# A trunk of two mixed-attention layers: first weights by row block, the memory rows' norm moved, forget parts earlier, last weave 8 to 6

## The chip, the core and the metric

The kernel runs on one core of a Trainium2 chip. TensorE (PE) multiplies matrices, VectorE (DVE) and ScalarE (ACT) work elementwise, GpSimd (POOL) does little here, and SyncE (SP) issues the DMAs. Each engine takes its instructions strictly in its own order; a semaphore holds one back until what it reads is there. The metric is the device time of one execution in microseconds (us); fewer is better.

## The reference

A hybrid decoder trunk with sequence 512 (T), model width 1024 (D) and two layers. In each layer:

```python
h = RMSNorm(x);  p = h @ w_in            # one projection, 10 kinds of heads and gates
y_a = DSA   (lightning-indexer top-k, gathered keys, low-rank KV, rotary)
y_b = FoX   (causal attention, logits + cum[t] - cum[s], cum = cumsum(log_sigmoid(p['fox_f'] + b)))
y_c = stick-breaking attention (sb_q, sb_k, sb_v)
y_d = NSA   (compressed / selected-block / window branches, gated)
y_e = cross-attention into mem: k, v = RMSNorm(mem) @ w_mem_kv     # 256 memory rows
merged = sum_n sigmoid(p['merge'][n]) * ((y_n * silu(z_n)) @ w_branch[n])
x = x + merged @ w_out
```

A last RMSNorm follows the two layers. Each branch has four heads of width 64; all is float32.

## The kernel before, in words

x lies transposed: 8 tiles of 128 features by 512 tokens. Each large projection is taken as three matmuls of a high and a low part (hi·hi, lo·hi, hi·lo; `mm3`, L261 to L264, all recorded at L259). So each weight block of 128x1024 (512 KB) is loaded into a buffer `wraw` (L278), split by ACT into `whi` (L269) and by DVE into `wlo` (L270). The raw buffers are a ring of two (tag "raw"), which the memory rows `mraw` (L1218) share with the weights.

A layer is written as generators: each `yield` ends a piece of work, and `weave` (L658) takes pieces in turn from several of them, the next one always from the generator whose pieces taken, divided by its number n, are fewest. `chain` runs generators one after another and `take` a few pieces of one. This order of writing and a priority decide how a scheduler lays out each engine's list; within a list nothing overtakes.

- The start of layer 0, `first` (L695) with `begin_tile` (L678): sb_q of the unnormed x, one tile after another: `u` and `ul` are the high and low parts of x times the norm's gain, `sq` its square, and the first weights are split by `start_split` (L707, ACT at L711, DVE at L712). Both weight blocks are 128x1024 and lie by column tile. Then `sumsq` and `rsqrt4` (a Newton iteration of twelve small DVE steps, L297 to L309), while sb_v's weights (ACT at L735, DVE at L736) are split.
- `memory_rows` (L375), layer 0 only: the memory rows' squares (ACT L336), seven adds (DVE L342), `ssq`, `rsqrt4`, `rowb` (PE L317) and the copy `rmem` (ACT L381). Layer 1 uses the same `rmem`. `mem_proj` (L1214) scales the rows by `rmem` (DVE L1222), splits them into `yhi` and `ylo` (L269, L270) and multiplies them with memk (two blocks) and memv (two).
- `small_proj` (L814): small heads; `smt_p` are transposes of rows of the tile `v` (L829), `sw_p` the rotary swap, then the logarithm of the forget gates (`fe`, `fu`, `forget_gates` L874).
- The stages (L1373 to L1400): stick-breaking pair 0 (`sb_attn(0)`, tiles `sbz`, `sp`, `Yc`) woven with the silu gate, the small projections and the memory projections; pair 1; then memory, NSA, DSA and FoX attention, each woven with the projections of the next and the merge of the branch before.
- `forget_rows` (L886), called once for each pair of FoX heads: splits the cumulative gates into `chi` and `clo`, loads a table `cbt` (L892), casts it to `sel` (ACT L894) and adds them to queries and keys by the matmuls `fox_e`.

Of the kernel before, what the change touches and what calls it, by code (L numbers as in the profile page):

```python
# [103 lines left out]
def _layout(x, mem, positions, norm_g, w_in, kv_norm, w_uk, w_uv, fox_bias, nsa_pe_k, nsa_pe_v,  # L104
# [82 lines left out]
def trunk(ctx: ExitStack, tc: tile.TileContext, xt, memt, pos, wall, small, vec, ca, cb, out):  # L187
# [32 lines left out]
    START_W = (1, 3)  # L220
    start_w = []
    for k in range(KT):
        nc.sync.dma_start(xs[:, k], xt[:, k])
        if k in START_W:
            r = wts.tile([128, 1024], F32, name="wraw", tag="raw", bufs=2)
            nc.sync.dma_start(r, wall[0, CH[('sb_q', 0)], :, 1024 * len(start_w):1024 * len(start_w) + 1024])
            start_w.append(r)
# [444 lines left out]
    def begin_layer(l):  # L672

        U = [wk.tile([128, 2, T], F32R, name="u", tag=t, bufs=2) for t in ("yhi", "yhi", "ylo", "ylo", "Z", "Z")]
        u = [x[:, e] for x in U for e in range(2)]
        return SimpleNamespace(uh=u[:KT], ul=u[KT:] + [slot("ul", F32R) for _ in range(2 * KT - len(u))], sq=[])

    def begin_tile(b, l, k, x, inorder=lambda e, ins: ins, middle=lambda k: None):  # L678

        sq = slot("sq")  # L680
        g = vcol(l * V_L + V_NG + k)
        inorder(0, nc.scalar.activation(b.uh[k], x, AF.Copy, scale=g))
        middle(k)
        inorder(0, nc.scalar.activation(sq, x, AF.Square))
        inorder(1, nc.vector.scalar_tensor_tensor(b.ul[k], x, g, f32(b.uh[k]), op0=OP.mult, op1=OP.subtract))
        if k == 0 or (l and k == KT - 1):
            b.sq.append(sq)
        else:
            inorder(1, nc.vector.tensor_add(b.sq[0], b.sq[0], sq))

    def layer(l, xs, begin):
# [3 lines left out]
        def first():  # L695
# [4 lines left out]
            if l == 0:  # L700
# [5 lines left out]

                def start_split(k):  # L707
                    if k in START_W:
                        w = [wts.tile([128, 1024], F32R, name="w", tag=t, bufs=3) for t in ("whi", "wlo")]
                        r = start_w[START_W.index(k)]  # L710
                        inorder(0, nc.scalar.activation(w[0], r, AF.Copy))  # L711
                        inorder(1, nc.vector.tensor_sub(w[1], r, f32(w[0])))  # L712
                        ws.append(w)
# [350 lines left out]
        def nsa_proj():  # L1064
# [22 lines left out]
            ht = sm.tile([64, 128], F32, name="ht", bufs=1)  # L1087
# [292 lines left out]
        if l == 0:  # L1380
            run(chain(memory_rows(), take(sp1, 1)))
# [3 lines left out]
            weave((sb_attn(0), 8), (chain(silu2('sb_z', lv.ZC), take(ixp, 1), take(sp1, 1), take(ixp, 1), mp), 10))  # L1385
# [12 lines left out]
        weave((fox_attn(), 16), (merge(0, lv.YA), 8))  # L1398
# [37 lines left out]
```

## Time and profile before

| | |
|---|---|
| median of 3 runs | 1337.55 us (1336.85 to 1339.21) |
| profiled execution, its span | 1338.58 us, 1336.8 us |
| mean granted clock of PE | 0.995 of full |
| busy: PE, DVE, ACT | 97%, 69%, 50% of the span |
| chain that ended last | PE 81%, ACT 9%, DVE 6%, issue 3%, DMA 1% |
| DMA | 124.10 MB, mean 93 GB/s |

Times in the timelines are us from the start of the span. In a row a tile's name stands for what is written, and after the arrow for what is read; matmuls overlap, so the distance of two starts says how fast they follow each other, not the length of one. An idle time in brackets is that of the engine before the row, with what ended it.

### The profile page before, as it was taken

What the parts mean: (1) busy time and instruction counts of PE and PEld (TensorE: products, weight loads), DVE (VectorE), ACT (ScalarE), POOL (GpSimd) and SP (SyncE); (2) the same over time, 40 slices, a digit from 0 to 9 for tenths busy, and PEclk for the clock granted to TensorE, in tenths of its full rate; (3) what the DMA queues carried; (4) which work ended last, traced back from release to release, by engine and by line L of the source; (5) the groups of instructions that cost most, each with busy time, mean ns of one, the idle gap of its engine ahead of it and who ended that gap; (6) DMA issues with size and microseconds to landing.
All of it is one profiled execution on the core that took longest, in us unless ns stands there. A gap on an engine that the chain in (4) does not pass through costs nothing.

```text
span 1336.8 us, 18894 instructions
## 1 busy us (share of the span) xinstructions
PE 1299.8 (97%) x7160; PEld 1066.1 (80%) x7160; DVE 916.1 (69%) x1983; ACT 675.0 (50%) x1260; POOL 42.5 (3%) x60
## 2 busy tenths in 40 slices
PE   7999999999999899999999999999999999999997
PEld 6777777878888788878887777778778878887896
DVE  6887999768655545644567799995686563465554
ACT  6887834357545424434447695534574452343340
POOL 0000011000000000000000001111000000000000
PEclk9999999999999999999999999999999999999998
DMA  6432321321223122223523213222122222323231
GB/s 222 135 127 79 103 90 62 95 78 60 65 78 103 55 95 79 69 83 130 184 88 126 96 63 127 79 70 89 49 78 63 88 87 69 100 81 99 95 111 63
DMA packets 40235, 124.10 MB, mean 93 GB/s; under 512 B 4432, under 2 KB 6480, under 8 KB 40144
## 3 DMA queue, kind: packets, MB, share of 16 engines
q1 hardware_dynamic: 40144, 122.89, 28.4%
q8 instruction: 56, 0.92, 0.3%
q14 instruction: 35, 0.29, 0.1%
HBM read 118.16 MB, written 4.72 MB: 92 GB/s over the span
## 4 chain that ended last, share of the span: by engine, by line
PE 81%; ACT 9%; DVE 6%; issue 3%; DMA 1%; SPq 0%; DVEq 0%; ACTq 0%
PE pj L259 67%; PE Y L259 4%; PE S L259 3%; PE pt L556 3%; ACT whi L269 2%; PE sbz L259 1%; DVE wlo L270 1%; ACT sw L430 1%; ACT Qi L854 1%; ACT sw L431 1%; ACT sp_t L388 1%; DVE Kl L456 0%; DVE rt L435 0%; DVE sw L434 0%; DMA wraw<-in_wall_dram 0%
## 5 line engine op out<-in xcount | busy, mean ns | idle before, releaser
L259 PE MATMUL pj<-h_hi,whi 128*128 128x512 f32 x1088 | 430.2, 397 | 1.1 <-DVE rt L433 1.1
L259 PE MATMUL pj<-h_lo,whi 128*128 128x512 f32 x1088 | 428.3, 394 | 0.0
L259 PE MATMUL pj<-h_hi,wlo 128*128 128x512 f32 x1088 | 426.7, 392 | 0.0
L270 DVE TENSOR_TENSOR wlo<-wraw,whi 128x1024 fp32r<-128x1024 f32 x183 | 223.6, 1222 | 216.8 <-ACT whi L269 205.9
L269 ACT ACTIVATE whi<-wraw 128x1024 fp32r<-128x1024 f32 x183 | 193.3, 1057 | 341.0 <-issue 170.7
L259 PEld LDWEIGHTS pj<-h_hi,whi 128*128 128x128 f32 x1088 | 204.5, 188 | 42.7 <-issue 2.4
L259 PEld LDWEIGHTS pj<-h_hi,wlo 128*128 128x128 f32 x1088 | 204.4, 188 | 42.7 <-DVE wlo L270 2.1
L259 PEld LDWEIGHTS pj<-h_lo,whi 128*128 128x128 f32 x1088 | 204.6, 188 | 41.9 <-issue 3.1
L547 ACT ACTIVATE P<-P,nm 128x128 f32<-128x128 f32 (+3 forms) x128 | 71.5, 559 | 64.8 <-DVE nm L546 64.1
L259 PE MATMUL pj<-yhi,whi 128*128 128x512 f32 (+1 forms) x192 | 71.9, 374 | 2.5 <-ACT yhi L269 2.3
L259 PE MATMUL pj<-yhi,wlo 128*128 128x512 f32 (+1 forms) x192 | 71.6, 373 | 0.0
L259 PE MATMUL pj<-ylo,whi 128*128 128x512 f32 (+1 forms) x192 | 71.5, 372 | 0.0
L546 DVE CUSTOM_DVE_ANT_0 P<-S,CA 128x128 f32<-128x128 f32 (+3 forms) x104 | 48.1, 466 | 32.3 <-PE S L259 32.3
L556 PE MATMUL pt<-CA,P 128*128 128x128 f32 x384 | 60.8, 278 | 2.4 <-DVE P L595 2.3
L556 PEld LDWEIGHTS pt<-CA,P 128*128 128x128 f32 x384 | 45.7, 143 | 13.4 <-issue 6.4
L259 PE MATMUL S<-Ks,Qs 128*128 128x256 f32 (+2 forms) x160 | 51.8, 365 | 4.1 <-DVE nm L546 4.0
L394 ACT ACTIVATE G<-pj 128x512 f32<-128x512 f32 x92 | 53.6, 583 | 1.5 <-PE pj L259 1.2
L908 DVE MATCH_REPLACE8 score<-m,score 128x256 f32<-128x256 f32 (+2 forms) x96 | 51.5, 540 | 0.0
L907 DVE MAX8 m<-score 128x8 f32<-128x256 f32 (+2 forms) x96 | 50.0, 546 | 0.0
L805 DVE SCALAR_TENSOR_TENSOR G<-G,pj 128x512 f32<-128x512 f32 x64 | 43.6, 681 | 3.5 <-PE pj L259 3.4
L806 DVE TENSOR_TENSOR acc<-acc,G 128x512 f32<-128x512 f32 x64 | 44.0, 687 | 0.8
L259 PEld LDWEIGHTS pj<-yhi,whi 128*128 128x128 f32 x192 | 36.1, 188 | 9.9 <-ACT yhi L269 3.7
(325 smaller groups left out, 2032.8 us busy)
## 6 DMA issues: line engine op xcount, KB each, us to landing
wraw<-in_wall_dram SPq DMA_DIRECT2D x192, 512.0 KB, 3.7
wc<-in_wall_dram SPq DMA_DIRECT2D x16, 256.0 KB, 6.1
x<-in_xt_dram SPq DMA_DIRECT2D x8, 256.0 KB, 5.8
mraw<-in_memt_dram SPq DMA_DIRECT2D x4, 512.0 KB, 4.4
xo<-in_xt_dram SPq DMA_DIRECT2D x8, 256.0 KB, 3.9
xspill<-xn SPq DMA_DIRECT2D x8, 256.0 KB, 2.1
xo<-xspill SPq DMA_DIRECT2D x8, 256.0 KB, 3.1
out_dram<-o SPq DMA_DIRECT2D x8, 256.0 KB, 2.2
```

Of the source, the lines that this page charges most:

```text
L259: return nc.tensor.matmul(out_, lhsT, rhs, start=start, stop=stop, **kw)
L269: nc.scalar.activation(hi, raw, AF.Copy)
L270: nc.vector.tensor_sub(lo, raw, hi.bitcast(F32))
L388: i = nc.scalar.activation(*a, **k)
L394: i = nc.scalar.activation(*a, **k)
L546: nc.vector.tensor_tensor_reduce(P, S, mask, -1.0, 3e38, OP.add, OP.min, nm)
L547: nc.scalar.activation(P, P, AF.Exp, bias=nm, scale=-1.0, accum_out=sums)
L556: nc.tensor.transpose(pt[:, 128 * j:128 * j + 128], x[:, c:c + 128], ident)
L805: nc.vector.scalar_tensor_tensor(G, G, gc, p, op0=gop, op1=OP.mult)
L806: nc.vector.tensor_add(acc, acc, G)
L907: nc.vector.max(m8, lv.work[i])
L908: nc.vector.match_replace(lv.work[i], m8, lv.work[i], REPL)
```

## The change

1. The first weight blocks are laid out by row block (both column tiles of a row block side by side) and loaded in four pieces of 128x512, the first from ACT's queue ahead of its table load, the others from SP between the tiles of x. They are split in the same pieces, ahead of u. In layer 0 a tile's square is taken after the next tile's u.
2. `memory_rows` of layer 0 moves from before the first weave into its chain, behind the second step of the small projections and ahead of `mem_proj`.
3. `forget_rows` is cut in two: `forget_parts`, written ahead of the projections of its pair, loads `cbt`, casts `sel` and, once a layer, splits `chi` and `clo`; `forget_rows` keeps the matmuls.
4. The last weave takes `merge(0)` with 6 in place of 8.
5. `smt_p`, `sw_p`, `hidT` work on 128 rows in place of 32 or 64; the gate of NSA's hidden layer is taken after its transpose.

```diff
         for a, b in PAIRS:
+            w2 = wall[l, CH[a]].reshape(128, 2, KT, 128)
+            if a == ('sb_q', 0):
+                w2 = wall[l, CH[a]].reshape(128, KT, 2, 128).transpose(0, 2, 1, 3)
...
+    start_w = [wts.tile([128, 1024], F32, name="wraw", tag="raw", bufs=2) for _ in range(2)]
+    def start_load(k):
+        c = slice(512 * (k % 4) // 2, 512 * (k % 4) // 2 + 512)
+        nc.scalar.dma_start(start_w[k // 4][:, c], wall[0, CH[('sb_q', 0)], :, 256 * k:256 * k + 512])
+    start_load(0)
+    nc.sync.dma_start(xs[:, 0], xt[:, 0])
+    nc.sync.dma_start(xs[:, 1], xt[:, 1])
+    nc.scalar.preload_act_table_set("exp_and_others")
+    for k in range(2, KT, 2):
+        c = slice(512 * (k % 4) // 2, 512 * (k % 4) // 2 + 512)
+        nc.sync.dma_start(start_w[k // 4][:, c], wall[0, CH[('sb_q', 0)], :, 256 * k:256 * k + 512])
+        for e in range(2):
+            nc.sync.dma_start(xs[:, k + e], xt[:, k + e])
...
     def begin_tile(b, l, k, x, inorder=lambda e, ins: ins, middle=lambda k: None):
+        middle(k)
         inorder(0, nc.scalar.activation(b.uh[k], x, AF.Copy, scale=g))
-        middle(k)
+        inorder(1, nc.vector.scalar_tensor_tensor(b.ul[k], x, g, f32(b.uh[k]), op0=OP.mult, op1=OP.subtract))
+        if l == 0:
+            b.rest.append((x, sq))
+            if k:
+                late_square(b, inorder)
+            return
...
             pt = bank("smt_p", "T")
             for i in range(NB):
-                nc.tensor.transpose(pt[:, 32 * i:32 * i + 32], lv.v2[fr, 128 * i:128 * i + 128], ident[fr, fr])
+                nc.tensor.transpose(pt[:, 128 * i:128 * i + 128], lv.v2[:, 128 * i:128 * i + 128], ident)
...
-        def forget_rows(pr):
-            chi = wk.tile([128, T], F32R, name="chi", tag="PT", bufs=5)
-            clo = wk.tile([128, T], F32R, name="clo", tag="PT", bufs=5)
-            split(lv.v2, chi, clo)
+        def forget_parts(pr):
+            if pr == 0:
+                lv.cs = slot("chi", F32R), slot("clo", F32R)
+                split(lv.v2, *lv.cs)
             cbt = slot("cbt")
             nc.sync.dma_start(cbt, cb[:, 512 + 512 * pr:1024 + 512 * pr])
-            sel = wk.tile([128, 512], F32R, name="sel", tag="G", bufs=3)
-            nc.scalar.activation(sel, cbt, AF.Copy)
+            lv.sel = slot("sel", F32R)
+            nc.scalar.activation(lv.sel, cbt, AF.Copy)
+        def forget_rows(pr):
+            (chi, clo), sel = lv.cs, lv.sel
...
             for pr in range(2):
+                forget_parts(pr)
                 yield from qk_pair('fox_q', pr, lv.QB, lv.KB, lv.KlB, lv.QlB)
                 forget_rows(pr)
...
-            run(chain(memory_rows(), take(sp1, 1)))
+            run(take(sp1, 1))
...
-            weave((sb_attn(0), 8), (chain(silu2('sb_z', lv.ZC), take(ixp, 1), take(sp1, 1), take(ixp, 1), mp), 10))
+            weave((sb_attn(0), 8), (chain(silu2('sb_z', lv.ZC), take(ixp, 1), take(sp1, 1), take(ixp, 1), memory_rows(), mp), 10))
...
-        weave((fox_attn(), 16), (merge(0, lv.YA), 8))
+        weave((fox_attn(), 16), (merge(0, lv.YA), 6))
```

First place: DVE, layer 0, around the copy of the small projection's transposes (`smt`). `mraw` are the memory rows being scaled, `ylo` their low parts. Before:

```order
95 L270 TENSOR_TENSOR ylo<-mraw,yhi 128x256 x2
96 L1222 SCALAR_TENSOR_TENSOR mraw<-mraw,VEC,rmem 128x256 x3
97 L456 TENSOR_TENSOR Ks<-pj,Ks 64x512
98 L964 SCALAR_TENSOR_TENSOR sp_t<-sbz,sp_t 128x512
99 L270 TENSOR_TENSOR ylo<-mraw,yhi 128x256
100 L980 CAST sp<-sp_t 128x512
101 L270 TENSOR_TENSOR ylo<-mraw,yhi 128x256
102 L981 TENSOR_TENSOR sp<-sp_t,sp 128x512
103 L830 COPY smt<-smt_p 128x128
104 L270 TENSOR_TENSOR wlo<-wraw,whi 128x1024
```

And after the change, from the same copy on:

```order
78 L857 COPY smt<-smt_p 128x128
79 L859 TENSOR_SCALAR wI<-smt 128x16
80 L455 TENSOR_TENSOR rt_751<-sw_p,sinI 32x512
81 L904 TENSOR_SCALAR fu<-v_627,VEC 32x512
82 L456 TENSOR_TENSOR rt_750<-rt_750,rt_751 32x512
83 L994 SCALAR_TENSOR_TENSOR sp_t<-sbz,sp_t 128x128
84 L1010 CAST sp<-sp_t 128x128
85 L1011 TENSOR_TENSOR sp<-sp_t,sp 128x128
86 L909 SCALAR_TENSOR_TENSOR fu<-fu,fe 32x512
87 L910 MEMSET fe 32x512
88 L352 TENSOR_TENSOR sq<-sq 128x256
89 L911 SCALAR_TENSOR_TENSOR v_627<-fe,fu 32x512
```

The adds of the squares (`sq`) begin ten entries behind the copy; the norm's twelve steps, the eight scalings and the eight `ylo` follow, and only then the next step of stick breaking and the first `wlo` of the memory weights, which stood right behind the copy before.

Second place: PE, the same stretch. `sbz` are stick-breaking scores, `pj<-yhi,...` the memory projection. Before:

```order
215 L829 MATMUL smt_p<-CA,v_684 128x32 x4
216 L259 MATMUL sw_p<-v_684,CA 32x512
217 L259 MATMUL sbz<-Qs,Ks 128x256 x2
218 L259 LDWEIGHTS identb
219 L259 MATMUL sbz<-sbm,identb 128x256
220 L259 MATMUL sbz<-sp,nones 128x256 x4
221 L259 MATMUL sbz<-sp,nones 128x384 x2
222 L259 MATMUL sbz<-sp,ntri 128x512 x2
223 L259 MATMUL pj<-yhi,whi 128x256
224 L259 MATMUL pj<-ylo,whi 128x256
```

After the change, where the same `sbz` rows stand behind the transposes and then:

```order
226 L269 MATMUL ssq<-ones_100,sq 128x1 x2
227 L327 MATMUL rowb<-CA,rs_y 128x128 x2
228 L269 MATMUL sbz<-Qs,Ks 128x256 x2
229 L269 LDWEIGHTS identb
230 L269 MATMUL sbz<-sbm,identb 128x128
231 L269 MATMUL sbz<-Qs,Ks 128x512 x2
232 L269 LDWEIGHTS identb
233 L269 MATMUL sbz<-sbm,identb 128x128
234 L269 MATMUL sbz<-sp,nones 128x256 x3
235 L269 MATMUL sbz<-sp,ntri 128x256
236 L269 MATMUL sbz<-sp,nones 128x256 x2
237 L269 MATMUL sbz<-sp,ntri 128x256
```

The sum of squares and the broadcast of the memory rows' norm stood inside the projections of 512 columns before (`rowb` at 162); now they stand between the stick-breaking scores, ahead of the first memory matmul (238).

Third place: PE in layer 0's DSA branch, where the second FoX pair's queries and keys are finished. `S`, `pt` and `Y` are scores, transposes and output of DSA's softmax, `pj<-yhi,whi` the merge of the branch before. Before:

```order
1741 L259 MATMUL S<-Ks,Qs 128x384 x2
1742 L556 MATMUL pt<-CA,P 128x128 x4
1743 L259 MATMUL S<-Ks,Qs 128x384 x4
1744 L259 MATMUL Y<-PT,VA 64x128 x8
1745 L556 MATMUL pt<-CA,P 128x128 x3
1746 L259 MATMUL S<-Ks,Qs 128x512 x2
1747 L556 MATMUL pt<-CA,P 128x128 x3
1748 L259 MATMUL S<-Ks,Qs 128x512 x2
1749 L556 MATMUL pt<-CA,P 128x128 x3
1750 L259 MATMUL S<-Ks,Qs 128x512 x4
1751 L556 MATMUL pt<-CA,P 128x128 x3
1752 L259 MATMUL fox_e<-chi,sel 128x512
```

After the change:

```order
1735 L269 MATMUL S<-Ks,Qs 128x384 x4
1736 L269 MATMUL pj<-yhi,whi 128x512
1737 L269 MATMUL pj<-ylo,whi 128x512
1738 L269 MATMUL pj<-yhi,wlo 128x512
1739 L269 MATMUL pj<-yhi,whi 128x512
1740 L269 MATMUL pj<-ylo,whi 128x512
1741 L269 MATMUL pj<-yhi,wlo 128x512
1742 L269 MATMUL Y<-PT,VA 64x128 x8
1743 L566 MATMUL pt<-CA,P 128x128 x2
1744 L269 MATMUL fox_e<-chi,sel 128x512
1745 L269 MATMUL fox_e<-clo,sel 128x512
1746 L566 MATMUL pt<-CA,P 128x128
```

Six merge matmuls, which stood ahead of the scores (1735 to 1740 before), stand between the scores and `Y`, and the `fox_e` pairs between the transposes.

## Rows read from the trace of the kernel before

**Rows 1.** The page: busy us, share of the span and instructions of each engine.

```profile
PE 1299.8 (97%) x7160; PEld 1066.1 (80%) x7160; DVE 916.1 (69%) x1983; ACT 675.0 (50%) x1260; POOL 42.5 (3%) x60
```

**Rows 2.** PE's waits: what waited for what, us in total, times, longest.

```profile
PE pj L259 <- ACT w L711: 8.8, 1, 8.8
```

**Rows 3.** Stretches: busy us of each engine, PE clock, DMA share, GB/s.

```profile
80.00:100.00 20.00, 18.88 (x134) 15.69 (x133) 17.13 (x29) 16.55 (x33) 0.00 (x0) 1.00 0.48 159
...
120.00:160.00 40.00, 39.02 (x187) 29.39 (x186) 38.66 (x78) 37.52 (x71) 0.65 (x1) 1.00 0.19 59
```

**Rows 4.** Timeline of the start: start us, length us, engine, line, instruction.

```profile
2.11 0.43 SPq L226 DMA_DIRECT2D wraw<-in_wall_dram  x1
...
4.44 0.72 ACT L682 ACTIVATE u<-x,VEC 128x512 fp32r<-128x512 f32 x1 [2.43 <-DMA x<-in_xt_dram]
...
7.72 1.06 ACT L711 ACTIVATE w<-wraw 128x1024 fp32r<-128x1024 f32 x1 [1.42 <-DMA wraw<-in_wall_dram]
...
8.82 9.05 PE L259 MATMUL pj<-u,w 128*128 128x512 f32 x25 [8.82 <-ACT w L711]
...
22.93 0.95 PE L259 MATMUL ssq<-ones,sq 128*128 128x1 f32 x8
```

**Rows 5.** Timeline of PE from the first stick-breaking scores to Yc.

```profile
62.10 0.33 PE L259 MATMUL sbz<-sbm,identb 128*128 128x256 bf16 x2 [0.71 <-ACT sbm L253]
...
74.21 0.39 PE L259 MATMUL pj<-h_lo,whi 128*128 128x512 f32 x1
74.43 0.39 PE L259 MATMUL pj<-h_hi,wlo 128*128 128x512 f32 x1
74.75 0.43 PE L829 MATMUL smt_p<-CA,v 32*128 32x32 f32 x4
...
97.14 2.37 PE L259 MATMUL Yc<-sb_a,VC 128*64 128x512 f32 x16
```

**Rows 6.** Timeline of DVE, memory rows and memory weights.

```profile
57.31 0.89 DVE L342 TENSOR_TENSOR sq<-sq 128x256 f32<-128x256 f32 x2
...
61.73 0.16 DVE L309 SCALAR_TENSOR_TENSOR rs_y<-rs_u,rs_y 128x2 f32<-128x2 f32 x1
...
64.57 1.27 DVE L1222 SCALAR_TENSOR_TENSOR mraw<-mraw,VEC,rmem 128x256 f32<-128x256 f32 x3
...
75.43 1.22 DVE L270 TENSOR_TENSOR wlo<-wraw,whi 128x1024 fp32r<-128x1024 f32 x1
...
79.64 0.41 DVE L270 TENSOR_TENSOR ylo<-mraw,yhi 128x256 fp32r<-128x256 f32 x1
...
89.20 1.23 DVE L270 TENSOR_TENSOR wlo<-wraw,whi 128x1024 fp32r<-128x1024 f32 x1
```

**Rows 7.** Timeline of ACT, the same stretch.

```profile
52.17 1.32 ACT L336 ACTIVATE sq<-memx 128x256 f32<-128x256 f32 x4
...
80.03 0.72 ACT L388 ACTIVATE fe<-fe,ones 32x512 f32<-32x512 f32 x1
...
84.03 1.07 ACT L269 ACTIVATE whi<-wraw 128x1024 fp32r<-128x1024 f32 x1
```

**Rows 8.** The page: DMA issues, KB each, median us from issue to landing.

```profile
wraw<-in_wall_dram SPq DMA_DIRECT2D x192, 512.0 KB, 3.7
```

**Rows 9.** Stretches behind the long waits of the DSA branch, columns as in rows 3.

```profile
446.00:448.40 2.40, 2.40 (x8) 1.96 (x7) 1.28 (x6) 1.49 (x4) 0.00 (x0) 0.50 0.00 0
...
1097.00:1100.40 3.40, 3.36 (x11) 2.50 (x12) 3.27 (x12) 3.09 (x8) 0.00 (x0) 0.50 0.30 77
```

**Rows 10.** Timeline of PE in layer 0, second FoX pair.

```profile
437.07 0.61 PE L259 MATMUL S<-Ks,Qs 128*128 128x384 f32 x2 [0.81 <-DVE nm L546]
...
443.93 0.52 PE L556 MATMUL pt<-CA,P 128*128 128x128 f32 x3 [1.53 <-DVE P L595]
```

**Rows 11.** Timeline of PE behind the FoX branch's last Y, layers 0 and 1.

```profile
574.28 0.50 PE L259 MATMUL pj<-yhi,whi 128*128 128x512 f32 x1 [1.27 <-ACT yhi L269]
...
1228.52 0.50 PE L259 MATMUL pj<-yhi,whi 128*128 128x512 f32 x1 [0.99 <-ACT yhi L269]
```

More of the change, by code (lines that the diff above doesn't have):

```diff
@@ L219, in trunk @@
     nc.sync.dma_start(VEC, vec)
[L220 to L227, printed above, removed]
+    start_w = [wts.tile([128, 1024], F32, name="wraw", tag="raw", bufs=2) for _ in range(2)]
[11 more added lines that the diff above has]
+            nc.sync.dma_start(xs[:, k + e], xt[:, k + e])
     CA = const.tile([128, 896], F32, name="CA")
@@ L438, in rope_index @@
     def rope_index(x, r, cosI, sinI):
-        p = bank("sw_p", "T")[r]
-        mm(p, perm[r, r], x[r], True, True)
+        p = bank("sw_p", "T")
+        mm(p, perm, x, True, True)
         t1 = slot("rt1")
@@ L675, in begin_layer @@
         u = [x[:, e] for x in U for e in range(2)]
-        return SimpleNamespace(uh=u[:KT], ul=u[KT:] + [slot("ul", F32R) for _ in range(2 * KT - len(u))], sq=[])
+        return SimpleNamespace(uh=u[:KT], ul=u[KT:] + [slot("ul", F32R) for _ in range(2 * KT - len(u))], sq=[], rest=[])
     def begin_tile(b, l, k, x, inorder=lambda e, ins: ins, middle=lambda k: None):
@@ L681, in begin_tile @@
         g = vcol(l * V_L + V_NG + k)
+        middle(k)
         inorder(0, nc.scalar.activation(b.uh[k], x, AF.Copy, scale=g))
-        middle(k)
+        inorder(1, nc.vector.scalar_tensor_tensor(b.ul[k], x, g, f32(b.uh[k]), op0=OP.mult, op1=OP.subtract))
[4 more added lines that the diff above has]
+            return
         inorder(0, nc.scalar.activation(sq, x, AF.Square))
-        inorder(1, nc.vector.scalar_tensor_tensor(b.ul[k], x, g, f32(b.uh[k]), op0=OP.mult, op1=OP.subtract))
-        if k == 0 or (l and k == KT - 1):
+        if k == 0 or k == KT - 1:
             b.sq.append(sq)
@@ L689, in begin_tile, with late_square @@
             inorder(1, nc.vector.tensor_add(b.sq[0], b.sq[0], sq))
+    def late_square(b, inorder):
+        x, sq = b.rest.pop(0)
+        inorder(0, nc.scalar.activation(sq, x, AF.Square))
+        if b.sq:
+            inorder(1, nc.vector.tensor_add(b.sq[0], b.sq[0], sq))
+        else:
+            b.sq.append(sq)
     def layer(l, xs, begin):
@@ L705, in inorder @@
                     prev[e] = ins
+                ws += [[wts.tile([128, 1024], F32R, name="w", tag=t, bufs=3) for t in ("whi", "wlo")] for _ in range(2)]
                 def start_split(k):
[L708 to L713, printed above, removed]
+                    if k % 2 == 0:
+                        c = slice(256 * (k % 4), 256 * (k % 4) + 512)
+                        hi, lo = (x[:, c] for x in ws[k // 4])
+                        r = start_w[k // 4][:, c]
+                        inorder(0, nc.scalar.activation(hi, r, AF.Copy))
+                        inorder(1, nc.vector.tensor_sub(lo, r, f32(hi)))
                 for k in range(KT):
                     begin_tile(b, 0, k, xs[:, k], inorder, start_split)
+                late_square(b, inorder)
                 state['start'] = prev[0], prev[1]
@@ L1085, in nsa_proj @@
             yield
-            ht = sm.tile([64, 128], F32, name="ht", bufs=1)
+            ht = sm.tile([128, 128], F32, name="ht", bufs=1)
             hid = bank("hid", "pj")[:, :128]
@@ L1118, in nsa_proj @@
             yield
-            hp = bank("hidT", "T")[:, :64]
-            nc.tensor.transpose(hp, ht, ident[0:64, 0:64])
+            hp = bank("hidT", "T")[:, :128]
+            nc.tensor.transpose(hp, ht, ident)
+            hs = sm.tile([128, 64], F32, name="hs", bufs=1)
+            nc.scalar.activation(hs, hp[:, 64:128], AF.Copy)
+            nc.vector.tensor_add(hs, hs, hp[:, 0:64])
+            gated(hs, hs, hs)
             hT = sm.tile([128, 32 * 5], F32, name="hT", bufs=1)
-            nc.scalar.activation(hT[:, 0:32], hp[:, 0:32], AF.Copy, scale=0.5)
-            nc.vector.tensor_scalar(hT[:, 32:160].rearrange("p (r n) -> p r n", n=32), hp[:, None, 32:64].to_broadcast([128, 4, 32]),
+            nc.scalar.activation(hT[:, 0:32], hs[:, 0:32], AF.Copy, scale=0.5)
+            nc.vector.tensor_scalar(hT[:, 32:160].rearrange("p (r n) -> p r n", n=32), hs[:, None, 32:64].to_broadcast([128, 4, 32]),
                                     0.5, None, op0=OP.mult)
```

17 lines of the change are left out of this document (7 added, 10 removed).

## The prediction, made before the changed kernel ran

> **What bounds the kernel now.** The page's first part comes first: TensorE (PE) is busy for 97% of the span [rows 1]. A change can therefore win only where PE stands still or runs at the lower clock, and it loses whatever new time PE stands still. The waits of PE come next: the longest single one is the first matmul's, 8.8 us, for ScalarE's (ACT's) split of the first weights [rows 2]. The table of stretches says who could take more work: from 80 to 100 us VectorE (DVE) is busy 17.1 of 20 us and ACT 16.6, and from 120 to 160 us PE, DVE and ACT are all above 37 of 40 [rows 3]. A delay made before 100 us is thus not won back in the next stage. The timelines then give the durations for each part. The profiled execution took 1338.58 us, 1.78 more than its span; it lies 1.03 us over the median of 1337.55, and I put the sum on the median.
>
> **The start.** Before, the first weights are issued third on SP's queue at 2.11 us, their split runs from 7.72 for 1.06 us, and the first matmul starts at 8.82; the 48 matmuls end at 22.93, where the sum of squares begins [rows 4]. Now a quarter of the bytes is asked for first, from ACT's queue. Its split takes half of 1.06 us, the first u another 0.72 [rows 4], so the first matmul can start near 5.3 us. The end is set by the eighth tile of x: ACT and DVE go through the tiles in the same pace from a start 3.5 us earlier (8.82 − 5.3), so the phase would end near 19.4. Not all of that arrives. In DVE's new order the two halves of sb_v's low weights stand behind the first step of the norm (rs_v), which waits for the sum of squares; before, the first stood ahead of it. With two steps of the rotary angles between, each half comes 1 us or so after PE wants it: some 2 us of new waiting. Term: −1.5 us, between −3.5 (order harmless) and +0.5 (first pieces no earlier).
>
> The Trainium skill ("DMA: Bandwidth & Descriptors", section "Issuing engines are not separate DMA queues") says that DMAs started from several engines run on the same 16 engines and save only issuing time. By that the second queue is worth about one issue, 0.4 us, and the start would give −1.1; no run here yet shows a load on ACT's queue.
>
> **The memory rows.** This is the largest term, and it goes against the change. Before, the norm of the memory rows runs between 52 and 64 us, and the scaling and splitting of the rows between 64 and 80, all under the projections of 512 columns. Call T0 the transposes of the small projection, at 74.75 us [rows 5]. At T0 + 0.7 the weights of the first memory projection are already being split, the last ylo ends at 79.64 + 0.41, T0 + 5.3, and the last memory weights (memv, second half) are split at 89.20 + 1.23, T0 + 15.7 [rows 6].
>
> Now all of this stands behind DVE's copy of the transposes, as the first order piece shows, and PE has the ssq and rowb matmuls in its own order ahead of every memory matmul, as the second shows. Step by step:
> - The squares stand on ACT behind fe's logarithm, which ended at 80.03 + 0.72, T0 + 6.0 [rows 7]. One weight split of 1.22 us no longer stands ahead of it on DVE, so T0 + 5.5. Eight squares at 0.33 (1.32 for four) [rows 7] end at T0 + 8.1.
> - Seven adds at 0.45 (0.89 for two) [rows 6], with the scan of the forget gates in between, end at T0 + 10.6.
> - From the last add to rs_y it was 58.20 to 61.89, with one foreign 0.69 us in it [rows 6]: 3.0, so T0 + 13.6. rowb's two small matmuls and the copy to rmem, of a square's size, end at T0 + 14.5.
> - Four scalings take 1.65 (1.27 for three) and four ylo at 0.35 to 0.41 some 1.4 [rows 6]: the first raw buffer is free at T0 + 17.8, the second at T0 + 20.8.
> - The weights share these two buffers. A load takes 3.7 us [rows 8], the high split 1.07 [rows 7] and the low one 1.23 [rows 6], together 6.2 with the hand-overs. Four loads on two buffers: memk at T0 + 24 and 27, memv at T0 + 30.3 and 33.5.
>
> Against T0 + 15.7 that is 17.8 us later, and what PE does after the last split (6.4 us to the Yc matmuls at 97.14 [rows 5]) is unchanged. PE has only a few us of stick-breaking scores in the meantime, and DVE's steps of these stand behind the chain too. Bounds: DVE alone must now do behind T0 adds 3.2, norm 2.3, scalings 3.3 and ylo 2.9, 11.7 us where 0.4 stood; if all of its idle time there, about 2 us of [rows 3], is filled, the loss is 9.5. If each of the four splits waits a further 1 us in its queue, it is 22. I take +18, near the step-by-step sum.
>
> The stretch before T0 gets lighter: the 0.71 us wait of the mask for its table at 62.10 [rows 5] goes, since the table is loaded ahead of the memory rows, and some matmul order with it. Term −1.0 (−1.5 to 0).
>
> Long waits also cost clock. After the waits around 444 us, PE's granted clock is 0.50, that is 1.2 GHz, from 446 to 448.4, and again from 1097 to 1100.4 [rows 9]. The gap behind T0 is longer than those. The small matmuls that lie in it wait for the chain anyway; only those behind its last wait count. Term +1, between 0 and +3.
>
> The Trainium skill ("TensorE: Matmul & The Clock Gate", section "HAM oscillation — how this bites in real kernels") holds that a loop which waits for data between bursts begins each burst throttled. The trace agrees, with 0.50 [rows 9]. By that rule each of the four waits for memory weights would be followed by a slow burst, and the term would be its upper end, +3.
>
> **The forget parts.** In layer 0 PE waits 0.81 us at 437.07 and 1.53 at 443.93 for the softmax of the DSA branch [rows 10], some 3.8 us in five waits between 436 and 444, and then runs 2.4 us at half the clock [rows 9]: 1.2 lost. As the third order piece shows, six merge matmuls (6 × 0.23 = 1.4 us at the step of [rows 5]) that stood ahead of the scores now stand behind them, and the four fox_e matmuls (0.9 us) are put between the transposes. Those 2.3 us fill waits, and if the clock then stays up it is 3.5, which I take; 5.0 would be all of it, 1 none of the clock and half the cover. Layer 1 has the same place at 1094 to 1100 with 3.4 us at 0.50 [rows 9]: −2.5. The two first fox_e pairs wait 0.2 each for sel: −0.4. Sum −6.4, between −11 and −2.
>
> **The last weave.** The last pieces of merge(0) now lie behind the fox branch's last Y. They cover the waits of 1.27 us at 574.28 and 0.99 at 1228.52 [rows 11]; each piece of 30 matmuls is 6.9 us of cover. −2.2, between −2.3 and 0.
>
> **Whole shapes.** The transposes and the swap for the small projection take whole rows with the same moving columns; a few small instructions of the NSA hidden layer move behind a transpose, under a projection of 24 matmuls, 5.5 us. 0, ±0.3; without that cover they would show as about 1 us.
>
> Sum: −1.5 −1.0 +18 +1 −6.4 −2.2 = +7.9, so 1337.55 + 7.9 = 1345.4; I say 1345.
>
> **Rivals.** A: *the chain runs at DVE's floor* and the gains come in full. For it: ACT has fewer entries between T0 and T0 + 15 than before, and the start and the fox stages have waits enough. Against it: squares, adds, norm and scaling wait for each other on three engines, so DVE can't fill its idle time. 9.5 −3.5 −1 −9 −2.2 = −6.2: 1331, faster than before. It decides if PE reaches the last memory weights by about T0 + 26.
> B: *the two sides cancel*: floor 9.5 against the gains that I take (11.1): −1.6, 1336, no change.
> C: *the clock goes with the gap*: 22 for the chain, 3 for the clock, start −1, pre-T0 −1, fox −2.5, weave −1: +19.5, 1357. For it: four separate waits for weights, each followed by a burst at 0.50 as in [rows 9]. Against it: ACT's and DVE's queues are short by then.
> D: *the fox cover isn't realised*, as the scores wait for the same softmax in any order: −2 in place of −6.4, +12.3, 1350. It is in the forecast's range.
>
> **How the numbers follow.** Forecast (with D) 0.50, A 0.20, B 0.16, C 0.14. About 0.2% (2.7 us) is what a measurement of this kernel can tell from no change: below 1334.9 faster, above 1340.2 slower. Faster takes A: 0.20. Same takes B: 0.16. Slower takes the forecast and C: 0.64. The likeliest case by itself reaches from 1340 to 1352; with half of A and most of C the range is 1332 to 1356.
>
> **What would show it.** In the profile after: the first matmul near 5.3 us and a wait for sb_v's low weights near 22; a gap of PE of 8 us or more behind the transposes, named rowb on rs_y, then waits on yhi, whi or wlo, and Yc some 38 to 42 us behind the transposes where it was 22.4; a granted clock under 1 there; the fox stretches at 1.00; no wait for yhi near the end of either fox branch. I am wrong if Yc comes within 32 us of the transposes, or if the stages up to 200 us, with DVE above 38 of 40 before [rows 3], turn out to have room to give the delay back.

## The result and the profile after

| | before | after |
|---|---|---|
| median (runs of the first comparison) | 1337.96 us (4 runs, 1336.85 to 1339.21) | 1350.36 us (4 runs, 1348.31 to 1352.54) |
| ratio after to before | | 1.0093, 95% interval 1.008 to 1.0105 |
| profiled run, its span | 1338.58, 1336.8 us | 1348.31, 1346.5 us |
| mean granted clock of PE | 0.995 | 0.989 |

The change makes the kernel slower by 12.4 us. The two profiled runs lie 9.73 us apart, as the profiled run of after is its shortest; of the others, 2 to 4 us longer, there is no trace. The run of added matmuls below has the same work up to the transposes of the small projection and reaches them at 74.39 us in place of 72.67, so a good part of that can lie between two executions of one kernel.

Milestones of PE's timeline, as starts in us, say where the time comes from:

| | before | after | difference |
|---|---|---|---|
| ssq of layer 0's first norm | 22.93 | 19.39 | −3.54 |
| rowb behind it | 30.42 | 28.48 | −1.94 |
| transposes of the small projection (smt_p) | 74.75 | 72.67 | −2.08 |
| Yc, first pair | 97.14 | 115.14 | +18.00 |
| hidT in the NSA projections | 196.66 | 214.58 | +17.92 |
| ssq of layer 1's first norm | 678.06 | 690.91 | +12.85 |
| Yc, layer 1, second pair | 807.30 | 820.42 | +13.12 |
| ssq of the final norm | 1301.19 | 1310.71 | +9.52 |

One stretch of 42 us loses 20.08 us; the start and the FoX ends of both layers give back the rest. Between Yc and hidT nothing is won back. PE's waits after (what waited for what, us in total, times, longest):

```profile
PE sbz L269 <- DVE sp_t L994: 7.1, 4, 5.1
PE ssq L269 <- DVE sq L352: 6.3, 1, 6.3
PE pj L269 <- ACT u L693: 6.0, 1, 6.0
PE rowb L327 <- DVE rs_y L319: 4.9, 2, 2.5
```

The wait of [rows 2] has shrunk from 8.8 to 6.0 us. In its place stand waits for DVE's sq, rs_y and sp_t, 18.3 us in all, of which 3.8 stood before, too (2.5 in one wait for rs_y, 1.3 in two for sp_t). The stretches (busy us of PE, PEld, DVE, ACT, POOL; then PE clock, DMA share, GB/s) show them in one place:

```profile
60.00:80.00 20.00, 17.60 (x86) 13.80 (x85) 9.66 (x19) 12.18 (x28) 0.51 (x2) 0.97 0.23 59
80.00:100.00 20.00, 7.59 (x32) 6.61 (x33) 16.42 (x47) 11.07 (x29) 0.71 (x3) 0.51 0.17 53
100.00:120.00 20.00, 18.18 (x128) 15.46 (x127) 11.27 (x15) 10.53 (x18) 0.00 (x0) 1.00 0.48 158
120.00:160.00 40.00, 39.67 (x185) 30.59 (x184) 32.90 (x58) 31.88 (x62) 0.00 (x0) 1.00 0.25 79
```

From 80 to 100 us PE is busy for 7.6 of 20 us at a clock of 0.51; in [rows 3] it was 18.9 at 1.00. DVE does 16.4 there, and had only 9.7 in the stretch ahead: work that DVE could have done from 60 to 80 is done from 80 to 100. From 120 to 160 PE is busy for 39.7 of 40: no room to win anything back. The Trainium skill ("TensorE: Matmul & The Clock Gate", section "HAM oscillation — how this bites in real kernels") says that PE comes out of a long wait for data at half rate. The trace agrees with its 0.51; what that costs is the question of an experiment below.

The start (timeline over all engines), against [rows 4]:

```profile
0.72 0.41 ACTq L227 DMA_DIRECT2D wraw<-in_wall_dram  x1
...
4.46 0.63 ACT L738 ACTIVATE w<-wraw 128x512 fp32r<-128x512 f32 x1 [2.01 <-DMA wraw<-in_wall_dram]
...
5.97 8.37 PE L269 MATMUL pj<-u,w 128*128 128x512 f32 x25 [5.97 <-ACT u L693]
...
19.39 0.95 PE L269 MATMUL ssq<-ones,sq 128*128 128x1 f32 x8
...
20.38 0.16 DVE L307 TENSOR_SCALAR rs_v<-ssq 128x4 f32<-128x4 f32 x1 [0.72 <-PE ssq L269]
...
21.13 1.22 DVE L763 TENSOR_TENSOR w<-wraw,w 128x1024 fp32r<-128x1024 f32 x1
...
22.40 1.57 PE L269 MATMUL pj<-w,u 128*128 128x256 f32 x11 [1.47 <-DVE w L763]
```

The first piece is asked for at 0.72 us from ACT's queue and split at 4.46; PE starts at 5.97, 2.85 earlier, and the sum of squares comes 3.54 earlier. Of these 3.54 us a part is spread between executions: in the five runs below that keep the old start it comes at 21.40 to 22.87 (here 22.93), in the seven others that have the new one at 19.61 to 20.43 (here 19.39). Then DVE reaches sb_v's low weights only behind rs_v, at 21.13, and PE waits 1.47 us for them.

PE behind the transposes, against [rows 5]:

```profile
72.67 0.60 PE L856 MATMUL smt_p<-CA,v 128*128 128x128 f32 x4
...
84.87 1.01 PE L269 MATMUL ssq<-ones,sq 128*128 128x1 f32 x4 [6.30 <-DVE sq L352]
88.30 0.69 PE L327 MATMUL rowb<-CA,rs_y 128*128 128x128 f32 x2 [2.42 <-DVE rs_y L319]
...
95.77 1.05 PE L269 MATMUL sbz<-sp,nones 128*128 128x256 f32 x3 [5.13 <-DVE sp_t L994]
...
108.10 0.38 PE L269 MATMUL pj<-wlo,yhi 128*128 128x256 f32 x1 [0.58 <-DVE wlo L280]
...
115.14 2.38 PE L269 MATMUL Yc<-sb_a,VC 128*64 128x512 f32 x16 [1.16 <-ACT sb_a L398]
```

PE waits 6.3, 2.4 and 5.1 us, and Yc comes 42.5 us behind the transposes in place of 22.4. DVE in the same stretch, against [rows 6]:

```profile
81.74 3.07 DVE L352 TENSOR_TENSOR sq<-sq 128x256 f32<-128x256 f32 x6
85.92 0.16 DVE L307 TENSOR_SCALAR rs_v<-ssq 128x2 f32<-128x2 f32 x1 [1.10 <-PE ssq L269]
...
88.08 0.16 DVE L319 SCALAR_TENSOR_TENSOR rs_y<-rs_u,rs_y 128x2 f32<-128x2 f32 x1
89.44 1.67 DVE L1255 SCALAR_TENSOR_TENSOR mraw<-mraw,VEC,rmem 128x256 f32<-128x256 f32 x4 [1.20 <-ACT rmem L391]
91.03 1.43 DVE L280 TENSOR_TENSOR ylo<-mraw,yhi 128x256 fp32r<-128x256 f32 x4
...
93.95 1.42 DVE L280 TENSOR_TENSOR ylo<-mraw,yhi 128x256 fp32r<-128x256 f32 x4
...
97.97 1.21 DVE L280 TENSOR_TENSOR wlo<-wraw,whi 128x1024 fp32r<-128x1024 f32 x1
...
106.83 1.22 DVE L280 TENSOR_TENSOR wlo<-wraw,whi 128x1024 fp32r<-128x1024 f32 x1 [0.79 <-ACT whi L279]
```

The adds end at 84.81 (T0 + 12.1 with T0 = 72.67), rs_y at 88.24, the last ylo at 95.37 (T0 + 22.7), and the low part of the last memory weights at 108.05 (T0 + 35.4). One entry after the other, the chain of the forecast.

The FoX stretches, against [rows 9] (columns as above):

```profile
450.00:462.00 12.00, 11.53 (x78) 9.27 (x77) 8.63 (x20) 7.80 (x15) 0.00 (x0) 1.00 0.25 76
...
1104.00:1112.00 8.00, 7.46 (x53) 5.66 (x52) 6.99 (x19) 6.65 (x16) 0.00 (x0) 1.00 0.21 68
```

PE is busy for 11.5 of 12 and 7.5 of 8 us, at 1.00 both times. No wait for yhi is left behind the last Y of either layer, where [rows 11] had 1.27 and 0.99.

### The profile page after: what moved, and what is told of

It reads as the page before. It is cut to its first block, busy times and chain, and to the rows that moved or that the text cites. A ratio compares the mean times of both kernels' runs of the same rounds, so it can differ in the third digit from the quotient of the medians.

```text
span 1346.5 us, 18912 instructions
## 1 busy us (share of the span) xinstructions
PE 1300.8 (97%) x7160; PEld 1066.9 (79%) x7160; DVE 914.7 (68%) x1983; ACT 674.5 (50%) x1262; POOL 41.8 (3%) x60
## 4 chain that ended last, share of the span: by engine, by line
PE 71%; DVE 5%; ACT 5%; issue 2%; POOL 0%; DVEq 0%; ACTq 0%
PE pj L269 58%; PE Y L269 4%; PE S L269 3%; PE pt L566 3%; ACT whi L279 1%; DVE wlo L280 1%; PE sbz L269 1%; DVE score L938 1%; DVE m L937 0%; ACT sw L441 0%; ACT sw L440 0%; ACT Qi L881 0%; DVE rt L445 0%; PE ssq L269 0%; ACT sp_t L398 0%
## 5 line engine op out<-in xcount | busy, mean ns | idle before, releaser
L556 DVE CUSTOM_DVE_ANT_0 P<-S,CA 128x128 f32<-128x128 f32 (+3 forms) x104 | 48.0, 466 | 33.2 <-PE S L269 33.2
```

What stands on the lines that cost most here:

```text
L556: nc.vector.tensor_tensor_reduce(P, S, mask, -1.0, 3e38, OP.add, OP.min, nm)
```

## The experiments

All are compared with runs of the kernel before on the same chip.

**The norm put back ahead of the first weave, all else as changed.**

```diff
-            run(take(sp1, 1))
+            run(chain(memory_rows(), take(sp1, 1)))
...
-            weave((sb_attn(0), 8), (chain(silu2('sb_z', lv.ZC), take(ixp, 1), take(sp1, 1), take(ixp, 1), memory_rows(), mp), 10))
+            weave((sb_attn(0), 8), (chain(silu2('sb_z', lv.ZC), take(ixp, 1), take(sp1, 1), take(ixp, 1), mp), 10))
```

> The whole change, but the memory rows' norm stands ahead of the first weave again, as before. Theory (the place of that norm is the loss): from the transposes of the small projection to Yc it is about 22.4 us as before and not 42.5, and the time falls by some 20 us below the changed kernel, to about 1327 us, 11 us under the kernel before: 1.9 of that from the start, 5.4 from layer 0's FoX part and last weave, 3.6 from layer 1's, as the milestones of the two traces have it. Rival (the other parts' new order costs something later that the memory wait hides now): 1334 to 1340 us, and Yc alone comes back.

Measured: 1335.19 us against 1338.32, ratio 0.9978 (0.9969 to 0.9987). That is the rival's range. The stretch behind the transposes is mended in part (79.81 to 105.30, 25.5 us), but the transposes come 5.1 us later than before. So with the norm at its old place the other parts together do not gain what the milestones above give them.

**The norm moved, all else as before.**

```diff
-            run(chain(memory_rows(), take(sp1, 1)))
+            run(take(sp1, 1))
...
-            weave((sb_attn(0), 8), (chain(silu2('sb_z', lv.ZC), take(ixp, 1), take(sp1, 1), take(ixp, 1), mp), 10))
+            weave((sb_attn(0), 8), (chain(silu2('sb_z', lv.ZC), take(ixp, 1), take(sp1, 1), take(ixp, 1), memory_rows(), mp), 10))
```

> The kernel before with one thing changed: the memory rows' norm stands behind the second step of the small projections, as in the changed kernel. Theory: the full 20 us, 1357 to 1358 us, Yc some 42 us behind the transposes, and next to nothing gained ahead of the transposes. Rival (the loss comes from the move together with the whole-row transposes or the earlier start): 1345 to 1350 us.

Measured: 1356.84 us against 1338.32, ratio 1.014 (1.0126 to 1.0154). PE's timeline:

```profile
73.89 0.43 PE L829 MATMUL smt_p<-CA,v 32*128 32x32 f32 x4
...
86.06 1.01 PE L259 MATMUL ssq<-ones,sq 128*128 128x1 f32 x4 [5.26 <-DVE sq L342]
89.50 0.69 PE L317 MATMUL rowb<-CA,rs_y 128*128 128x128 f32 x2 [2.42 <-DVE rs_y L309]
...
96.97 1.05 PE L259 MATMUL sbz<-sp,nones 128*128 128x256 f32 x3 [5.13 <-DVE sp_t L964]
...
116.47 2.37 PE L259 MATMUL Yc<-sb_a,VC 128*64 128x512 f32 x16 [0.90 <-ACT sb_a L388]
```

Yc stands 42.6 us behind the transposes, with the same three waits: the move alone, on the old rows of 32, costs all of it.

**The norm in the same chain, two steps earlier.**

```diff
-            weave((sb_attn(0), 8), (chain(silu2('sb_z', lv.ZC), take(ixp, 1), take(sp1, 1), take(ixp, 1), memory_rows(), mp), 10))
+            weave((sb_attn(0), 8), (chain(silu2('sb_z', lv.ZC), memory_rows(), take(ixp, 1), take(sp1, 1), take(ixp, 1), mp), 10))
```

> The changed kernel, with the memory rows' norm in the same chain but two steps earlier, right behind the silu gate and ahead of both small projections. In the changed kernel DVE is busy for only 9.7 of the 20 us from 60 to 80. Theory (what counts is being behind the transposes and the forget gates on DVE and ACT): the norm is done by about 65 us, Yc 22 to 26 us behind the transposes, 1326 to 1331 us. Rival (any place inside the weave puts the chain into the stick-breaking steps' way): Yc 30 us or more behind the transposes, 1336 us or more.

Measured: 1337.55 us against 1338.32, ratio 0.9994 (0.9985 to 1.0002). PE's timeline:

```profile
59.34 0.38 PE L269 MATMUL sbz<-sbm,identb 128*128 128x256 bf16 x3 [2.50 <-ACT sbm L263]
...
80.17 0.60 PE L856 MATMUL smt_p<-CA,v 128*128 128x128 f32 x4
```

From the transposes to Yc (103.64) it is 23.5 us, as the theory says: ahead of the transposes the norm costs nothing behind them. But the transposes come 5.4 us late: PE waits 2.50 for the mask's cast, and its granted clock is 0.57 from 60 to 64 us behind that. The total is the rival's.

**Buffers of their own for the memory rows.**

```diff
-            for j in range(2):
-                mx_ = wts.tile([128, 4, NM], F32, name="mraw", tag="raw", bufs=2)
...
+            for j in range(4):
+                mx_ = wts.tile([128, 2, NM], F32, name="mraw", tag="mraw", bufs=2)
...
```

> The changed kernel, but the memory rows to be scaled have two buffers of their own (four loads of 256 KB in place of two of 512 KB), so the weights don't wait for the raw buffers that they shared. Theory: of the 42.5 us from the transposes to Yc the part in which four weight loads follow the chain one by one on two buffers goes: the first two memory weights are split before the chain ends, and Yc comes at about 35 us, 1343 to 1345 us. Rival (the order of DVE alone is the loss, the ring is none): Yc at 41 to 43, 1349 to 1351 us. The two late loads of memory rows can cost 2 to 3 us of what is won.

Measured: 1344.95 us against 1338.32, ratio 1.0051 (1.0039 to 1.0064). PE's timeline:

```profile
74.52 0.60 PE L856 MATMUL smt_p<-CA,v 128*128 128x128 f32 x4
...
110.44 1.93 PE L269 MATMUL Yc<-sb_a,VC 128*64 128x512 f32 x9
```

Yc comes after 35.9 us. So of the 20 us some 6.6 are the ring of two raw buffers, which the rows hold until the chain is done. The other 13.5 are left, by subtraction, to the order of the lists; no run takes them apart further.

**The new start alone.** Edit: the first three pieces of the change's diff (layout, loads, late squares) on the kernel before.

> The kernel before with the new start alone (row blocks, four pieces, squares a tile late). In PE's list the memory rows' ssq then stands at row 122 in place of 144, as in the run with the norm put back, which had new waits of 2.0 us (ssq) and 2.3 us (Qs) there and Yc 8.2 us later than before. Theory (the start moves the first 3.5 us up, but its list pulls the memory norm ahead of its data, and the delay stays): Yc at about 105 us, the end 4 to 5 us later than before, 1342 to 1343 us. Rival (those waits come from the whole-row transposes, or from the forget parts): the start gives its 1.9 us, 1336 us.

Measured: 1342.76 us against 1338.13, ratio 1.0038 (1.0025 to 1.005). First PE, then DVE:

```profile
55.35 0.74 PE L269 MATMUL ssq<-ones,sq 128*128 128x1 f32 x4 [2.03 <-DVE sq L352]
58.38 0.76 PE L269 MATMUL pj<-h_hi,whi 128*128 128x512 f32 x1 [2.29 <-DVE Qs L468]
58.94 0.63 PE L269 MATMUL pj<-h_lo,whi 128*128 128x512 f32 x1
```

```profile
51.06 3.07 DVE L352 TENSOR_TENSOR sq<-sq 128x256 f32<-128x256 f32 x6
54.16 0.68 DVE L468 SCALAR_TENSOR_TENSOR Qs<-pj,Qs 64x512 fp32r<-64x512 f32 x1
54.87 0.43 DVE L352 TENSOR_TENSOR sq<-sq 128x256 f32<-128x256 f32 x1
56.13 0.16 DVE L307 TENSOR_SCALAR rs_v<-ssq 128x2 f32<-128x2 f32 x1 [0.83 <-PE ssq L269]
56.21 1.23 DVE L280 TENSOR_TENSOR wlo<-wraw,whi 128x1024 fp32r<-128x1024 f32 x1
57.35 0.16 DVE L309 TENSOR_SCALAR rs_a<-rs_v 128x2 int32<-128x2 int32 x1
57.54 0.69 DVE L468 SCALAR_TENSOR_TENSOR Qs<-pj,Qs 64x512 fp32r<-64x512 f32 x1
```

The first ssq comes 3.0 us earlier (19.92), the transposes 5.2 later (79.98). As the memory norm's ssq stands further ahead in PE's list (row 122 in place of 144), PE reaches it 2.03 us before DVE's adds are done, though these end 2.9 us earlier than before; one Qs step of 0.68 stands between them. Then rs_v waits for ssq, the second Qs stands behind rs_v and a weight split, and PE waits 2.29 for Qs. Behind these waits PE's granted clock is 0.50 from 56 to 62 us: nine matmuls of 512 columns from 58.4 to 62.6 follow each other at 0.43 us where [rows 5] has 0.22, some 2 us more. The two waits and these 2 us are 6.3 of the 6.6 us lost between rowb (29.02, before 30.42) and the transposes. The start was the only edit, so it is with the start that the scheduler laid these lists out anew.

**The forget parts alone.** Edit: `forget_parts` and its call, as in the change's diff.

> The kernel before with the forget parts early alone. Theory: the merge and fox_e matmuls fill the softmax waits of layer 0's and layer 1's DSA branch and the clock stays at 1.00 there: 4 us less in layer 0, 2.5 in layer 1, 1331 to 1332 us. Rival (the waits are only moved behind the fox_e matmuls, or the gain in the whole change came from the weave): 1335 to 1338 us.

Measured: 1330.81 us against 1338.13, ratio 0.9949 (0.9936 to 0.9961): the theory, and a little more.

**The weave alone.**

```diff
-        weave((fox_attn(), 16), (merge(0, lv.YA), 8))
+        weave((fox_attn(), 16), (merge(0, lv.YA), 6))
```

> The kernel before with the last weave's 8 made 6 alone. Theory: the two waits for yhi of 1.27 and 0.99 us go and nothing else, 1336 us (2.2 less). Rival (the merge pieces are missing as cover inside the fox branch, where they stood before): 1338 us or more.

Measured: 1336.68 us against 1338.13, ratio 0.9992 (0.9984 to 1.0001): the right size, but by its interval not told from no change.

**Both FoX parts, nothing else.**

> The kernel before with the two parts that act behind 400 us: the forget parts early and the weave at 6; no new start, no moved norm, no whole rows. Theory (these are all the gains of the change but the start's): about 5.4 us less in layer 0 and 3.6 in layer 1, 1329 us, faster than both kernels. Rival (they share one gain): 1332 us or more.

Measured: 1328.3 us against 1338.13, ratio 0.9933 (0.992 to 0.9947). This version beats both kernels; it was the fastest of all that ran.

**Matmuls into the gap.** Edit: in `memory_rows` of the changed kernel, eight `mm(wp, perm, iq, ...)` ahead of ssq and ten `mm(wp[:, :NM], perm, rmem, ...)` behind rowb, into a bank that nobody reads (16 and 20 in the trace).

> The changed kernel with matmuls put on PE into the gap behind the transposes whose result nobody reads: eight of 512 columns ahead of the memory rows' ssq and ten of 256 columns behind rowb, so that PE does not stand still there. Theory (the norm's chain on DVE and ACT sets the end; the clock at 0.51 from 80 to 100 us costs only what stands behind the last wait): PE's granted clock there is near 1, ssq, rowb and the stick-breaking scores take half as long, and Yc comes 1 to 2.5 us earlier, 40 to 41.5 us behind the transposes, 1348 to 1349 us. Rival (the clock is a large part of the loss): Yc at 36 us or less, under 1345 us. If the added matmuls delay a score that DVE waits for, Yc does not get earlier at all.

Measured: 1351.45 us against 1338.11, ratio 1.0097 (1.0083 to 1.011); the changed kernel had 1.0093. The stretch, then PE:

```profile
80.00:100.00 20.00, 16.12 (x60) 11.11 (x58) 15.32 (x44) 10.76 (x30) 1.22 (x4) 0.83 0.09 26
```

```profile
74.39 0.60 PE L868 MATMUL smt_p<-CA,v 128*128 128x128 f32 x4
...
86.30 0.60 PE L269 MATMUL ssq<-ones,sq 128*128 128x1 f32 x4 [1.94 <-DVE sq L352]
...
89.32 0.69 PE L327 MATMUL rowb<-CA,rs_y 128*128 128x128 f32 x2 [0.24 <-DVE rs_y L319]
...
90.90 5.79 PE L269 MATMUL warm<-rmem,CA 128*128 128x256 f32 x20
96.34 0.58 PE L269 MATMUL sbz<-Qs,Ks 128*128 128x512 f32 x1
...
112.79 1.08 PE L269 MATMUL Yc<-sb_a,VC 128*64 128x512 f32 x4 [0.65 <-ACT sb_a L409]
...
118.06 1.51 PE L269 MATMUL Yc<-sb_a,VC 128*64 128x384 f32 x12
```

The clock is 0.83 in place of 0.51, and ssq takes 0.60 in place of 1.01 us. ssq stands 11.9 us behind the transposes (12.2 without the added matmuls) and rowb 14.9 (15.6); Yc begins at 38.4, but its larger part comes at 43.7.

Of the 0.7 us up to rowb only 0.3 are the clock's: rs_v's wait for ssq is 0.78 us in place of 1.10. The other 0.4 come from ACT's list, in which the squares begin at T0 + 5.6 in place of T0 + 6.0 (T0 are the transposes). At rowb the clock is 0.50 again, and rmem's copy follows it after 0.73 us as without the added matmuls (0.72; 0.41 in the kernel before). So an estimate from these rows is 0.6 us of clock up to rmem.

Behind rowb the run decides less than it seems to: the second batch of added matmuls holds the next scores back to 96.34 (T0 + 22; without the batch they stand ahead of T0 + 18), ACT waits 1.86 us for them ahead of the last yhi, and the last memory weights are split by T0 + 38.2 in place of T0 + 35.4. That the end does not move is thus no proof that the clock costs nothing there. The changed kernel's own trace says more: from rmem's copy on, DVE's scalings and ylo (89.44 to 95.37) follow each other without a wait for PE, and from 100 to 120 us PE's clock is 1.00 again. The rival, 36 us or less from the transposes to Yc, did not come.

**The norm written ahead of the weave, behind the second pair's step.**

```diff
-            run(take(sp1, 1))
+            run(chain(take(sp1, 1), memory_rows()))
...
-            weave((sb_attn(0), 8), (chain(silu2('sb_z', lv.ZC), take(ixp, 1), take(sp1, 1), take(ixp, 1), memory_rows(), mp), 10))
+            weave((sb_attn(0), 8), (chain(silu2('sb_z', lv.ZC), take(ixp, 1), take(sp1, 1), take(ixp, 1), mp), 10))
```

> The changed kernel, but the memory rows' norm is written ahead of the first weave again, behind the step of the second stick-breaking pair in place of ahead of it. In PE's list ssq then stands at 151 (before: 144; with the norm put back ahead of that step: 122). Theory (the new start costs time only because it pulls ssq and the queries' steps ahead of their data): no new waits there, the start keeps its 1.9 us, with 9.8 us of the FoX parts 1326 to 1328 us, faster than the run with forget parts and weave alone (1328.3). Rival (the start's loss is in the list anyhow): 1332 to 1336 us.

Measured: 1337.41 us against 1338.11, ratio 0.9996 (0.9987 to 1.0005). The theory fails: ssq stands at row 151, yet PE waits 2.8 us for its adds, and the transposes come at 79.14. It is not ssq's row alone. Behind the wait PE's granted clock falls to 0.50 (64 to 68 us); from 60 to 80 it is 0.83:

```profile
60.00:80.00 20.00, 17.65 (x75) 14.19 (x76) 14.62 (x45) 13.56 (x34) 1.22 (x4) 0.83 0.12 35
```

**That, with sb_v's first splits at a higher priority.**

```diff
-                    after(nc.scalar.activation(w[half][0], r, AF.Copy), state['start'][0])
-                    after(nc.vector.tensor_sub(w[half][1], r, f32(w[half][0])), state['start'][1])
+                    with tc.high_priority(offset=3000):
+                        after(nc.scalar.activation(w[half][0], r, AF.Copy), state['start'][0])
+                        after(nc.vector.tensor_sub(w[half][1], r, f32(w[half][0])), state['start'][1])
```

> As the run with the norm behind the pair, and the splits of sb_v's first weights get a higher priority, so that DVE's list has the first of them ahead of the norm's first step (rs_v), as the kernel before had. Theory (PE's wait of 1.5 us for these low weights near 22 us is the part of the start that was lost): 1.5 us less, 1325 to 1326 us. Rival (the wait only moves to the broadcast of the norm behind it): no difference to it, within 0.5 us.

Measured: 1334.89 us against 1338.11, ratio 0.9972 (0.9961 to 0.9984). It is 2.5 us less than the run before, where the theory had 1.5 and the rival nothing. The wait for sb_v's low weights is gone and rowb comes at 27.63 (28.72 without the priority): 1.1 us. PE still waits for the memory rows' adds, as long as without the priority:

```profile
60.54 0.61 PE L269 MATMUL ssq<-ones,sq 128*128 128x1 f32 x4 [2.76 <-DVE sq L352]
```

But here its clock stays at 1.00 behind the wait. The same 70 matmuls from ssq up to the transposes (74.56) take 14.02 us; in the run before they took 16.79, at a mean clock of 0.80. So 2.8 of the 4.65 us between the two profiled executions (1334.01 and 1338.66) are the clock's. Why it fell behind one wait of 2.8 us and not behind the other isn't shown, and how much of the 2.5 us between the medians is the priority's stays open beyond the 1.1.

**The whole shapes alone.** Edit: the pieces of the change on smt_p, sw_p and hidT.

> The kernel before with the whole shapes alone (smt_p, sw_p and hidT on 128 rows, the NSA gate behind its transpose). Theory: nothing, 1338 us within 0.5. Rival (the gate behind the transpose is a new wait for PE, or the list around the transposes changes): 1339 us or more.

Measured: 1339.24 us against 1338.11, ratio 1.001 (1.0001 to 1.0019): the rival's side, by 1.1 us, and only just clear of no change. hidT stands at 196.71 (before 196.66), the end of the span 0.6 later; where it is lost isn't shown.

## Why the prediction was right

The direction, the main term and the place were right; 1350.4 lies in the range (1332 to 1356), 5.4 us over the predicted 1345, and Yc's 42.5 us is half a microsecond above the "38 to 42" named. The range also holds rivals B and D; the trace, more than the number, speaks for the forecast.

- **Memory rows, +18 and clock +1**: measured 20.08 from the transposes to Yc. That the place of the norm is the cause is shown by its own run (+18.5); the chain is read from the trace. The mis-sized step is the middle of the chain: adds and norm ended at T0 + 15.6, where 13.6 was forecast, since fe's logarithm ended at T0 + 6.0 and not 5.5, the seven adds took 0.51 each in a row, and ssq 1.01 us. These 2 us ran through to the last split (T0 + 35.4 against 33.5). Yc then waited 1.2 more for sb_a. The gap has its forecast size but not its names: PE waits for sq, rs_y and sp_t (6.3, 2.4 and 5.1 us), where rs_y and then yhi, whi or wlo were named. Two slips in the working are small: PE's stretch from the last split to Yc was 6.7 us before (97.14 − 90.43), not 6.4, and T0 + 27 and a load of 6.2 make T0 + 33.2, not 33.5. Of the clock's +1, 0.3 us was measured at ssq, and the estimate up to rmem is 0.6; what of it reaches Yc isn't shown. Its upper end of +3, a slow burst behind each of four waits for weights, did not come: PE's one wait for memory weights was 0.58 us, and the clock was 1.00 from 100 us on.
- **The ring of raw buffers**, in the sum as "four loads on two buffers", is 6.6 us of it, by the run with buffers apart.
- **The start, −1.5**: −1.94 at rowb in the profiled pair, for the reason given: 3.54 won, 1.6 lost again behind rs_v. That it fits so well is partly luck. The first matmul came at 5.97 and not at 5.3, and the pair is the late end of the old start and the early end of the new one: over all profiled runs the medians at rowb are 30.1 (six with the old start) and 29.0 (seven with the new one, without the raised priority), 1.1 us apart. What the prediction lacked: the parts are not independent. With the norm at its old place the start costs 4.6 us, because the lists around it change; in the whole change the moved norm takes these waits away. The sum of the single runs (start +4.6, norm +18.5, forget −7.3, weave −1.5, shapes +1.1) is +15.4; 12.4 was measured.
- **Ahead of the transposes, −1.0**: −0.14 (from −1.94 to −2.08). PE still waits for the mask, 0.47 us here and 1.37 with the added matmuls, and the stretch was nearly full before.
- **FoX −6.4 and weave −2.2**: in the trace −5.1 in layer 0 (from +17.92 to +12.85) and −3.6 in layer 1 (from +13.12 to +9.52), 8.7 in place of 8.6; alone, both parts give 9.8. So D, no cover for the softmax, fell, though its 1350 is the measured time.
- **Whole shapes, 0**: about +1 in their own run, outside the ±0.3 given.
- A (DVE at its floor) and B fell: DVE was idle behind T0 in waits of 1.53, 1.10 and 1.20 us, as the argument against A said. C (the clock) fell as the four slow bursts did not come.
- Of the 2.7 us between 9.7 in the profiled pair and 12.4 in the medians, up to 1.7 can be the early transposes of the profiled run of after (72.67; 74.39 in the run with added matmuls). The rest is not explained.

## What to carry to other kernels

When work is moved from a busy place to one "behind" another step, look at what stands behind it on each of its engines: here seven adds and twelve tiny steps, harmless under projections, became 20 us once PE's next matmuls and two shared buffers waited for them. Time each part of a bundle alone: here two of five parts gained 9.8 us together, and each of the other three cost time by itself. Where a scheduler lays out the lists, a part's price depends on the others, so a sum of single effects is a guess until the bundle is read in the trace. And one profiled execution is one draw: milestones of the start differ by 1 to 2 us between runs that share its code.

## What the runs showed of the hardware that was not expected

The first split of weights began at 4.46 us in place of 7.72. Its load was issued 1.39 us earlier (0.72 against 2.11) and had half the bytes; the other 1.9 us of the 3.26 came with the smaller piece and its place ahead of x, which no run took apart. The Trainium skill ("DMA: Bandwidth & Descriptors", section "Issuing engines are not separate DMA queues") says that a second issuing engine saves only the time to issue. The 1.39 us are of that kind: on SP the load stood behind three issues of 0.39 to 0.45 us each.

Keeping PE busy through most of the gap raised its granted clock from 0.51 to 0.83 from 80 to 100 us. The end did not move, but the added matmuls also held scores back, so this alone does not price the clock.

What a gap costs through the clock depends on what stands behind it. Behind the norm's wait of 2.8 us stood projections that waited for nothing else, and the same 70 matmuls took 16.79 us at 0.80 in one run and 14.02 at 1.00 in another.
